# Router tables summed six pieces later, the last two weight pieces multiplied unsplit, two experts' rows fetched by one transfer, six loads moved to SyncE

## The chip, the cores and the metric

One core of a Trainium2 chip runs the kernel; the other cores are idle. The metric is device time in microseconds, the median of several executions.

## The reference, cut to what matters

Two blocks of a network for 512 tokens of width 1024, all in fp32. The first is a modulated norm, a wide projection, a retention branch and a convolution branch, and an output projection. The second is sliding-window attention beside a gated unit, cross attention to a memory of 256 rows, and a mixture of 32 experts. The change touches the second block, most of all its experts:

```python
def hierarchical_moe(h, w_router_group, w_router_expert, w1, w3, w2):
    ...
    p_group = jax.nn.softmax(xf @ w_router_group, axis=-1)      # 4 groups
    g_idx = jnp.argmax(p_group, axis=-1)
    ...
    top_logit, top_idx = lax.top_k(local, TOP_K)                # 2 of the group's 8 experts
    gate = jax.nn.softmax(top_logit, axis=-1) * g_w[:, None]
    ...
    def run_block(args):                                        # each expert on its own tokens
        xblk, e = args
        hid = jax.nn.silu(xblk @ w1[e]) * (xblk @ w3[e])
        return hid @ w2[e]
    ...
    y = jnp.zeros((T + 1, D)).at[slot_tok].add(yb * slot_w[:, None])[:T]
```

## The kernel before, in words

**Products.** An fp32 operand is cut into a high and a low part: ScalarE casts (`wh`, lines 151 and 1270), VectorE subtracts (`wl`, lines 152 and 1273), and TensorE (PE) multiplies the parts (`mm`, line 143). SyncE (SP) issues the weight loads, mostly 1 MB each, in the order of use, and issues one as soon as the buffer it goes to is free.

**Attention stage.** Around 780 to 930 us the kernel loads small tables on GpSimd's queue: a row of gains `rows` (line 823), the gate's bias `sgb` (826) and matrices `sgw` (828). GpSimd then multiplies `sgw` by a triangle in four steps (line 831). Between these it takes reciprocal roots `rs` for the norms (line 227), for which VectorE waits. Further loads on its queue are a gain row (975), `cqg` (1034), the router's weights `wr` (1102), and zeros written behind the output (1130). In this stage a scheduler of the framework places the instructions of GpSimd and the other engines.

**Experts.** From about 1050 us on each of 32 experts has three matrices of 2 MB (`w1`, `w3`, `w2`), each cut into four pieces. The list `pieces` runs w1 ×4, w3 ×2, w2 of the expert before ×2, w3 ×2, w2 ×2. One load (`piece_load`) brings two pieces into a slot of a ring of nine. The loop at line 1684 takes one piece `i` after the other; `prepare` loads and splits 5, then 4, and near the end 3 pieces ahead. One piece of each `w1` (`whole`, line 1541) is not split but multiplied in fp32 by `up_whole`. `after(i, d, f)` queues a function for the end of piece `i + d`. From here on the code's order is every compute engine's order (`manual_schedule`).

An expert has up to 64 tokens here (`CAP` per pass; overflow goes to a loop behind, which stays as it is). Tokens and gates of each expert are put into tables in DRAM by eight indirect scatters of GpSimd (`table`, line 1508, at piece 4), read back by four transfers (`table_back`, line 1513, at piece 11), and summed by six VectorE instructions (`table_sum`, lines 1518 to 1525, at piece 18) into gates `tg` and token numbers `ti`. The first four experts don't need them: their rows are picked by small matmuls. For expert 4 and later GpSimd fetches the 64 rows by one indirect transfer (`fetch`, line 1638, into one of the two buffers of `rows`, tile X4); PE turns them (`turn`, `s_turn`, line 230); ScalarE and VectorE split them (`s_parts`). `down` multiplies by `w2`; `combine` weighs the result (lines 1574 and 1575) and GpSimd adds it to the output by an indirect transfer (line 1576), each of which waits until the one before has landed.

```python
        if i == 18:
            table_sum()
...
            if c == 1 and NE <= e + 1 < 32:
                after(i, 0, lambda e=e: s_turn(e + 1))
                after(i, 1, lambda e=e: s_parts(e + 1))
            if c == 3 and NE <= e + 2 < 32:
                after(i, 0, lambda e=e: s_fetch(e + 2))
```

Of the kernel before, what the change touches and what calls it, by code (L numbers as in the profile page):

```python
# [111 lines left out]
def build(tc, I, out):  # L112
# [712 lines left out]
    sgb = ap_.tile([128, 8], F32, name="sgb")  # L825
    G.dma_start(sgb, I["sgbt"])
    sgw = ap_.tile([128, 8, 128], F32, name="sgw")
    G.dma_start(sgw, I["sgwt"])
    for j in range(4):
# [144 lines left out]
    g_out = alt("gain")  # L974
    G.dma_start(g_out, I["onorm"].to_broadcast([128, D]))
    mT = []
# [56 lines left out]
    cqg = ap_.tile([128, 256], F32, name="cqg")  # L1033
    G.dma_start(cqg, I["rows"][:, 648:].to_broadcast([128, 256]))
    oT = []
# [65 lines left out]
    wr = alt("gain", (128, KT, 40))  # L1101
    G.dma_start(wr, I["wr"])
    for k in range(KT):
# [25 lines left out]
    V.memset(zero[:64], 0.0)  # L1129
    G.dma_start(out[T:T + 64, :], zero[:64])  # L1130

# [383 lines left out]
    def table_sum():  # L1515

        t = rows[:64, 1, 512:512 + CAP]
        V.tensor_reduce(t, rows[:64, 1, :NT * CAP].rearrange("p (m v) -> p v m", m=NT), AX.X, OP.add)
        t = t.rearrange("p (e v) -> p e v", v=2)
        for l in range(2):  # L1520
            V.tensor_copy(tg[l * 64:l * 64 + 64], t[:, :, 1])
        u = rows[:64, 1, 640:672]
        V.tensor_scalar(u, t[:, :, 0], 0.0, float(1 << 20), OP.is_equal, OP.mult)
        V.scalar_tensor_tensor(u, t[:, :, 0], 1.0, u, op0=OP.subtract, op1=OP.add)
        V.tensor_copy(ti[:64], u)


# [13 lines left out]
    def whole(i):  # L1541

        n, e, c = pieces[i]
        return n == "w1" and (c == 2 or e == 0 and c == 3)

    def down(yb, hd, f, w):

        for q in range(2):
            mm(yb[q], hd[:, f], w[1][:, q, :], f == 0, False)
            mm(yb[q], hd[:, f], w[0][:, q, :], False, f == 3)  # L1550

    def add_parts(b, aS, q):
# [87 lines left out]

    def turn(x):

        b = pget("pg")
        for k in range(KT):
            transpose(b[:, k * 64:k * 64 + 64], x[:, k * 128:k * 128 + 128])
        return b.rearrange("p (k s) -> p k s", k=KT)
# [5 lines left out]
    def s_fetch(e):  # L1652
        fetch(rows[:64, e % 2], ti[:64, e:e + 1])

    def s_turn(e):
        st[e]["xb"] = turn(rows[:64, e % 2])

# [26 lines left out]
    for i, (n, e, c) in enumerate(pieces):  # L1684
# [14 lines left out]
        if i == 4:  # L1699
            rows = lp.tile([128, 2, D], F32, name="X4")  # L1700
            G.memset(rows[:64], 0.0)
            table()
        if i == 11:
            g.finish()
            table_back()
        if i == 18:
            table_sum()
        if n != "w2":
            if c == 0:
                s_[n] = pget("pa")  # L1710
            if whole(i):
                up_whole(s_[n], s_["xg"], 2 * c, raw_of[i])
            else:
                up(s_[n], s_["xg"], 2 * c, split_of.pop(i))
        else:
            if c == 0:
                s_["y"] = [pget("pg" if e == 31 else "py") for _ in range(2)]
            down(s_["y"], s_["hd"], c, split_of.pop(i))
        raw_of.pop(i)
        if c == 3:  # L1720
# [14 lines left out]
        if n == "w1" and e < 32:  # L1735
            if c == 1 and NE <= e + 1 < 32:
                after(i, 0, lambda e=e: s_turn(e + 1))
                after(i, 1, lambda e=e: s_parts(e + 1))
            if c == 3 and NE <= e + 2 < 32:
                after(i, 0, lambda e=e: s_fetch(e + 2))  # L1740
        for f in late.pop(i, ()):
# [15 lines left out]
    with tc.For_i(0, nv, 1):  # L1757
# [22 lines left out]
        fetch(rows[:64, 0], ga.ii[:, 0:1])  # L1780
        parts(turn(rows[:64, 0]), ga.xg[0])
        w1, w3, w2 = (I[n][bass.ds(ev, 1)].rearrange("o k n -> (o k) n") for n in ("w1_2", "w3_2", "w2_2"))
# [44 lines left out]
```

## Time and profile before

| | |
|---|---|
| runs | 1702.79, 1703.10, 1703.52 us, median 1703.1 |
| profiled execution | 1703.71 us, of which its span (first to last instruction) 1701.9 |
| PE busy | 1620.8 us (95%), weight loads 1265.4 beside |
| VectorE (DVE) busy | 1269.3 us (75%) |
| ScalarE (ACT) busy | 876.4 us (51%) |
| GpSimd (POOL) busy | 200.7 us (12%) |
| granted PE clock | 0.984 of full speed over the span |
| DMA | 338 MB, 202 GB/s over the span |

The busy shares are means over unlike stages, so they are read together with the page's 40 slices: there PE is at nine or more tenths almost everywhere, the DMA engines reach nine tenths from about 1200 us on, and there is one slice (the 28th, 1149 to 1191 us) in which the granted clock shows 7. Idle time in a row, "[9.89 <-DMA X<-slots]", stands before that instruction on its engine and names what ended it.

### The profile page before, as it was taken

Reading aid. Unit: us, or ns where it says so; the run is one execution under the profiler, and the core shown is the slowest. Engines: PE = TensorE matmul, PEld = TensorE weight load, DVE = VectorE, ACT = ScalarE, POOL = GpSimd, SP = SyncE. Lnnn points to the kernel's source line nnn. Section 1 sums busy time; section 2 is a strip of 40 time slices with the busy share of each in tenths; the row PEclk is TensorE's granted clock in tenths of the full one; section 3 lists DMA queues with packets and bytes.
Section 4 is the critical chain, followed back from the end, with each engine's and each line's share of the span. In section 5 each row is a group of like instructions: output and inputs, shape, how many; then the busy total and the mean of one; then the engine's idle time right before and its main releaser. Section 6 shows DMA issues by size and latency. Waiting matters only on the chain.

```text
span 1701.9 us, 20349 instructions
## 1 busy us (share of the span) xinstructions
PE 1620.8 (95%) x7587; PEld 1265.4 (74%) x7587; DVE 1269.3 (75%) x1809; ACT 876.4 (51%) x1299; POOL 200.7 (12%) x179
## 2 busy tenths in 40 slices
PE   8999999999999999999899999987999999999994
PEld 6888888888888878887787877865666666666663
DVE  5969996479994374446765554476999999998995
ACT  6533232322222334344554343356888888887884
POOL 1100100000100000004101010015112122121211
PEclk9999999999999999999999999997999999999997
DMA  9932222223222262334121331466999999999992
GB/s 342 322 104 96 97 93 99 83 91 112 79 99 89 91 230 100 118 123 142 50 75 66 112 98 50 161 228 222 381 395 403 399 394 399 389 398 394 393 368 60
DMA packets 101316, 338.02 MB, mean 199 GB/s; under 512 B 9601, under 2 KB 27329, under 8 KB 76896
## 3 DMA queue, kind: packets, MB, share of 16 engines
q1 hardware_dynamic: 90272, 308.76, 48.3%
q0 software_dynamic: 9504, 23.65, 4.9%
q10 hardware_dynamic: 1440, 4.31, 0.7%
q8 instruction: 60, 0.98, 0.2%
q14 instruction: 40, 0.33, 0.1%
HBM read 327.29 MB, written 17.11 MB: 202 GB/s over the span
## 4 chain that ended last, share of the span: by engine, by line
issue 21%; PE 17%; DMA 16%; DVE 5%; POOL 2%; ACT 2%; POOLq 0%; ACTq 0%; DVEq 0%
DMA out_dram<-xs,ti 13%; PE pmm L143 8%; PE ps L143 4%; PE ppv L143 2%; DMA out_dram<-xs,ii 2%; PE psc L143 2%; POOL rs L227 1%; PE ptr L230 1%; DMA slots<-dat,pi 0%; POOL sgw L831 0%; DMA adg<-in_w_ada_dram 0%; DVE X L755 0%; DVE xs L1180 0%; DVE wl L152 0%; DVE xs L765 0%
## 5 line engine op out<-in xcount | busy, mean ns | idle before, releaser
L151 ACT CAST wh<-raw 128x1024 fp32r<-128x1024 f32 x174 | 182.0, 1051 | 393.3 <-PE ps L143 341.6
L152 DVE TENSOR_TENSOR wl<-raw,wh 128x1024 fp32r<-128x1024 f32 x174 | 211.8, 1220 | 173.2 <-ACT wh L151 172.3
L143 PE MATMUL pmm<-wl,xr 128*128 128x512 f32 x388 | 175.6, 453 | 12.2 <-DVE wl L1273 10.3
L143 PE MATMUL pmm<-wh,X 128*128 128x512 f32 (+1 forms) x544 | 179.5, 401 | 0.3 <-DVE qn L858 0.3
L143 PE MATMUL ps<-hH,wl 128*128 128x512 f32 x448 | 176.1, 394 | 0.0
L143 PE MATMUL ps<-hL,wh 128*128 128x512 f32 x448 | 174.6, 390 | 0.0
L143 PE MATMUL ps<-hH,wh 128*128 128x512 f32 x448 | 174.5, 389 | 0.0
L491 DVE SCALAR_TENSOR_TENSOR cvo<-apad,cw,cvo 128x512 f32<-128x512 f32 x240 | 169.2, 743 | 0.9
L1273 DVE TENSOR_TENSOR wl<-X,wh 128x1024 fp32r<-128x1024 f32 x138 | 161.4, 1220 | 4.3 <-ACT wh L1270 4.0
L143 PE MATMUL pmm<-wh,xr 128*128 128x512 f32 x388 | 154.3, 398 | 0.0
L1270 ACT CAST wh<-X 128x1024 fp32r<-128x1024 f32 x138 | 138.1, 1053 | 5.6 <-DMA X<-in_w_dram 4.3
L143 PE MATMUL ps<-wl,hH 128*128 128x512 f32 x320 | 124.6, 390 | 0.0
L1273 DVE TENSOR_TENSOR wl<-raw,wh 128x1024 fp32r<-128x1024 f32 x104 | 121.6, 1220 | 3.9 <-ACT wh L1270 3.6
L143 PE MATMUL ps<-wh,hH 128*128 128x512 f32 x320 | 124.5, 390 | 0.0
L143 PE MATMUL ps<-wh,hL 128*128 128x512 f32 x320 | 124.5, 390 | 0.0
L143 PEld LDWEIGHTS pmm<-wl,xr 128*128 128x128 f32 x388 | 73.7, 190 | 61.6 <-DVE wl L1273 42.5
L143 PEld LDWEIGHTS pmm<-wh,X 128*128 128x128 f32 x544 | 102.1, 191 | 20.2 <-DVE qn L858 0.4
L143 PE MATMUL pmm<-wl,X 128*128 128x512 f32 (+1 forms) x272 | 108.4, 399 | 0.0
L1270 ACT CAST wh<-raw 128x1024 fp32r<-128x1024 f32 x104 | 104.3, 1052 | 5.2 <-DMA raw<-in_w_dram 5.0
L1576 POOL DMA_INDIRECT out_dram<-xs,ti x27 | 61.5, 2276 | 355.5 <-DVE xs L1575 355.5
L143 PEld LDWEIGHTS ps<-hH,wl 128*128 128x128 f32 x448 | 84.6, 189 | 17.5 <-issue 0.2
L143 PEld LDWEIGHTS ps<-hL,wh 128*128 128x128 f32 x448 | 84.3, 188 | 17.7 <-issue 0.2
(450 smaller groups left out, 3300.7 us busy)
## 6 DMA issues: line engine op xcount, KB each, us to landing
X<-in_w_dram SPq DMA_DIRECT2D x81, 1024.0 KB, 12.3
raw<-in_w_dram SPq DMA_DIRECT2D x63, 1024.0 KB, 11.9
raw<-in_w_in_dram SPq DMA_DIRECT2D x43, 1024.0 KB, 4.9
pre<-in_w_dram SPq DMA_DIRECT2D x42, 1024.0 KB, 11.9
adar<-in_w_ada_dram SPq DMA_DIRECT2D x16, 512.0 KB, 8.1
raw<-in_w_in_dram SPq DMA_DIRECT2D x16, 512.0 KB, 4.5
raw<-in_w_ret_out_dram SPq DMA_DIRECT2D x8, 1024.0 KB, 4.9
raw<-in_w_out_dram SPq DMA_DIRECT2D x8, 1024.0 KB, 5.0
```

The source lines that it names most:

```text
L143: PE.matmul(o, l, r, start=start, stop=stop)
L151: A.copy(hi, src)
L152: E.tensor_sub(lo, src, hi.bitcast(F32))
L227: G.tensor_tensor(o, o, mhalf[:, :w], op=OP.pow)
L230: PE.transpose(o, i, ident[:i.shape[0], :i.shape[0]])
L491: V.scalar_tensor_tensor(st["o"], ap[:, j:j + T], cw[:, k, j:j + 1], st["o"], op0=OP.mult, op1=OP.add)
L1270: A.copy(split_of[i][0], raw_of[i])
L1273: E.tensor_sub(split_of[i][1], raw_of[i], split_of[i][0].bitcast(F32))
L1576: G.indirect_dma_start(out=out, out_offset=bass.IndirectOffsetOnAxis(ap=idx[:, :1], axis=0), in_=y[:64, :], in_offset=None, bounds_check=T ...
```

## The change

1. `table_sum` runs at piece 24, not 18. A seventh instruction in it writes the token numbers of experts 1 to 31, one column to the left, into partitions 64 to 127 of `ti`.
2. With that, one indirect transfer of 128 rows brings the rows of experts `e` and `e + 1` (`e` even): one transfer every second expert in place of one each. The odd expert's rows lie in partitions 64 to 127 and are turned from there. A pair's buffer is used alternately, as an expert's was. The first one is issued at the end of piece 24. The clearing of `rows` covers 128 partitions.
3. The last two pieces of the last expert's `w2` are not split; when both are there, `down_whole` multiplies them in fp32, by output half.
4. Six loads and writes of GpSimd's queue (lines 826, 828, 972, 1034, 1102, 1130 before) go to SP's.

On DVE, in the experts' stage, before (`X_8731` is the tile `rows`, `jk` belongs to the bookkeeping of overflow, `wl` and `gain` are low parts of weights):

```order
L1273 TENSOR_TENSOR wl_8932<-X_8921,wh_8931 128x1024
L1518 TENSOR_REDUCE X_8731<-X_8731 64x64
L1521 COPY tg<-X_8731 64x32 x2
L1523 TENSOR_SCALAR X_8731<-X_8731 64x32
L1524 SCALAR_TENSOR_TENSOR X_8731<-X_8731 64x32
L1525 CAST ti<-X_8731 64x32
L1672 COPY jk<-psc 32x128
L1673 TENSOR_SCALAR jk<-jk 32x128
L1675 SCALAR_TENSOR_TENSOR jk<-jk 32x128 x6
L1273 TENSOR_TENSOR wl_8974<-pre_8963,wh_8973 128x1024
```

and with the change:

```order
L1687 COPY npre<-psc 128x33
L1688 CAST nblk<-npre 128x1
L1273 TENSOR_TENSOR wl_9013<-raw_9010,wh_9012 128x1024
L1273 TENSOR_TENSOR wl_9021<-raw_9010,wh_9020 128x1024
L1518 TENSOR_REDUCE X_8731<-X_8731 64x64
L1521 COPY tg<-X_8731 64x32 x2
L1523 TENSOR_SCALAR X_8731<-X_8731 64x32
L1524 SCALAR_TENSOR_TENSOR X_8731<-X_8731 64x32
L1525 CAST ti<-X_8731 64x32
L1526 CAST ti<-X_8731 64x31
L1273 TENSOR_TENSOR wl_9044<-raw_9041,wh_9043 128x1024
```

The overflow's bookkeeping, five weight splits and an expert's `hidden` and `combine` now stand ahead of the sum.

On POOL, in the experts' stage, before (`X_8731<-xscr` is the fetch of rows, `out_dram<-xs` the sum into the output):

```order
L1638 DMA X_8731<-xscr,ti 64x1024
L1576 DMA out_dram<-xs_9274,ii 576x1024
L1638 DMA X_8731<-xscr,ti 64x1024
L1576 DMA out_dram<-xs_9421,ii 576x1024
L1638 DMA X_8731<-xscr,ti 64x1024
```

and with the change:

```order
L1583 DMA out_dram<-xs_8982,ii 576x1024
L1645 DMA X_8731<-xscr,ti 128x1024
L1583 DMA out_dram<-xs_9128,ii 576x1024
L1583 DMA out_dram<-xs_9272,ii 576x1024
L1645 DMA X_8731<-xscr,ti 128x1024
L1583 DMA out_dram<-xs_9419,ii 576x1024
```

A fetch of 128 rows follows every second sum into the output.

On POOL, in the attention stage (a difference; `sgw` and `sgb` belong to the gated unit, `rs` are norms' roots, `gain_6769` is the gain row of the output norm):

```order
 L823 DMA rows<-in_rows_dram 128x904
-L826 DMA sgb<-in_sgbt_dram 128x8
-L828 DMA sgw<-in_sgwt_dram 128x1024
+L831 TENSOR_TENSOR sgw<-sgw,cst 128x256 x3
 L227 TENSOR_TENSOR rs_5787<-rs_5787,mhalf 128x1
 L227 TENSOR_TENSOR rs_5837<-rs_5837,mhalf 128x1
-L831 TENSOR_TENSOR sgw<-sgw,cst 128x256 x4
-L975 DMA gain_6769<-in_onorm_dram 128x1024
+L831 TENSOR_TENSOR sgw<-sgw,cst 128x256
 L227 TENSOR_TENSOR rs_5928<-rs_5928,mhalf 128x2
```

Three of the four multiplications of `sgw` now stand ahead of two roots. The loads reappear on SP between weight loads.

The diff:

```diff
@@ -823,9 +823,9 @@
     G.dma_start(rows, I["rows"].to_broadcast([128, 904]))
     qg, kg, sink, sgn = rows[:, :64], rows[:, 64:128], rows[:, 128:136], rows[:, 136:648]
     sgb = ap_.tile([128, 8], F32, name="sgb")
-    G.dma_start(sgb, I["sgbt"])
+    nc.sync.dma_start(sgb, I["sgbt"])
     sgw = ap_.tile([128, 8, 128], F32, name="sgw")
-    G.dma_start(sgw, I["sgwt"])
+    nc.sync.dma_start(sgw, I["sgwt"])
     for j in range(4):
         js = slice(2 * j, 2 * j + 2)
         G.tensor_mul(sgw[:, js], sgw[:, js], cst[:, None, C_SGU:C_SGU + 128].to_broadcast([128, 2, 128]))
@@ -972,7 +972,7 @@
         us.append(u)
     ws = block([W2[:, 1280:1792]])
     g_out = alt("gain")
-    G.dma_start(g_out, I["onorm"].to_broadcast([128, D]))
+    nc.sync.dma_start(g_out, I["onorm"].to_broadcast([128, D]))
     mT = []
     for m in range(NT):
         b = pmm()
@@ -1031,7 +1031,7 @@
     vS = ap_.tile([128, 2, D], F32, name="vS")
     nc.sync.dma_start(vS.rearrange("p a b -> p (a b)"), vscr)
     cqg = ap_.tile([128, 256], F32, name="cqg")
-    G.dma_start(cqg, I["rows"][:, 648:].to_broadcast([128, 256]))
+    nc.sync.dma_start(cqg, I["rows"][:, 648:].to_broadcast([128, 256]))
     oT = []
     for nb in range(2):
         ws = block([I["w_cq_2"][:, nb * 512:nb * 512 + 512]])
@@ -1099,7 +1099,7 @@
     V.tensor_copy(trib[:, :128], cst[:, C_TRI:C_TRI + 128])
     V.tensor_copy(trib[:, 128:], onesf)
     wr = alt("gain", (128, KT, 40))
-    G.dma_start(wr, I["wr"])
+    nc.sync.dma_start(wr, I["wr"])
     for k in range(KT):
         V.tensor_scalar(wr[:, k, :], wr[:, k, :], vcol("norm_ffn_2", k), None, OP.mult)
     iota32 = cst[:, C_E32:C_E32 + 32]
@@ -1127,7 +1127,7 @@
     g_ffn = gain(I["gffn"])
     zero = alt("xs")
     V.memset(zero[:64], 0.0)
-    G.dma_start(out[T:T + 64, :], zero[:64])
+    nc.sync.dma_start(out[T:T + 64, :], zero[:64])
 
     for m in range(NT):
         nc.sync.dma_start(slots[m].rearrange("(p s) v -> p (s v)", p=64), zero[:64, :CAP])
@@ -1523,6 +1523,7 @@
         V.tensor_scalar(u, t[:, :, 0], 0.0, float(1 << 20), OP.is_equal, OP.mult)
         V.scalar_tensor_tensor(u, t[:, :, 0], 1.0, u, op0=OP.subtract, op1=OP.add)
         V.tensor_copy(ti[:64], u)
+        V.tensor_copy(ti[64:, :31], u[:, 1:])
 
 
     def up(b, x, k0, w):
@@ -1541,13 +1542,19 @@
     def whole(i):
 
         n, e, c = pieces[i]
-        return n == "w1" and (c == 2 or e == 0 and c == 3)
+        return n == "w1" and (c == 2 or e == 0 and c == 3) or n == "w2" and e == 31 and c > 1
 
     def down(yb, hd, f, w):
 
         for q in range(2):
             mm(yb[q], hd[:, f], w[1][:, q, :], f == 0, False)
             mm(yb[q], hd[:, f], w[0][:, q, :], False, f == 3)
+
+    def down_whole(yb, hd, fs, ws):
+
+        for q in range(2):
+            for f, w in zip(fs, ws):
+                mm(yb[q], hd[:, f].bitcast(F32), w[:, q, :], False, f == 3)
 
     def add_parts(b, aS, q):
 
@@ -1638,11 +1645,11 @@
         G.indirect_dma_start(out=o, out_offset=None, in_=xscr, in_offset=bass.IndirectOffsetOnAxis(ap=ids, axis=0),
                              bounds_check=T - 1, oob_is_err=False)
 
-    def turn(x):
+    def turn(x, p):
 
         b = pget("pg")
         for k in range(KT):
-            transpose(b[:, k * 64:k * 64 + 64], x[:, k * 128:k * 128 + 128])
+            PE.transpose(b[:, k * 64:k * 64 + 64], x[p:p + 64, k * 128:k * 128 + 128], ident[p:p + 64, p:p + 64])
         return b.rearrange("p (k s) -> p k s", k=KT)
 
     def parts(b, xg):
@@ -1650,10 +1657,10 @@
         V.tensor_sub(xg[:, :, 64:], b, xg[:, :, :64].bitcast(F32))
 
     def s_fetch(e):
-        fetch(rows[:64, e % 2], ti[:64, e:e + 1])
+        fetch(rows[:, e // 2 % 2], ti[:, e:e + 1])
 
     def s_turn(e):
-        st[e]["xb"] = turn(rows[:64, e % 2])
+        st[e]["xb"] = turn(rows[:, e // 2 % 2], e % 2 * 64)
 
     def s_parts(e):
         st[e]["xg"] = xgs.next()
@@ -1698,12 +1705,12 @@
             gates()
         if i == 4:
             rows = lp.tile([128, 2, D], F32, name="X4")
-            G.memset(rows[:64], 0.0)
+            G.memset(rows, 0.0)
             table()
         if i == 11:
             g.finish()
             table_back()
-        if i == 18:
+        if i == 24:
             table_sum()
         if n != "w2":
             if c == 0:
@@ -1715,8 +1722,12 @@
         else:
             if c == 0:
                 s_["y"] = [pget("pg" if e == 31 else "py") for _ in range(2)]
-            down(s_["y"], s_["hd"], c, split_of.pop(i))
-        raw_of.pop(i)
+            if not whole(i):
+                down(s_["y"], s_["hd"], c, split_of.pop(i))
+            elif c == 3:
+                down_whole(s_["y"], s_["hd"], (2, 3), (raw_of[i - 1], raw_of[i]))
+        if not (n == "w2" and e == 31 and c == 2):
+            raw_of.pop(i)
         if c == 3:
             if n == "w1":
                 after(i, 1, lambda e=e: s_copy1(e))
@@ -1736,8 +1747,8 @@
             if c == 1 and NE <= e + 1 < 32:
                 after(i, 0, lambda e=e: s_turn(e + 1))
                 after(i, 1, lambda e=e: s_parts(e + 1))
-            if c == 3 and NE <= e + 2 < 32:
-                after(i, 0, lambda e=e: s_fetch(e + 2))
+            if c == 3 and e % 2 == 0 and NE <= e + 2 < 32:
+                after(i, 1 if e == 2 else 0, lambda e=e: s_fetch(e + 2))
         for f in late.pop(i, ()):
             f()
     p8.close()
@@ -1778,7 +1789,7 @@
         ga.start()
         ga.finish()
         fetch(rows[:64, 0], ga.ii[:, 0:1])
-        parts(turn(rows[:64, 0]), ga.xg[0])
+        parts(turn(rows[:, 0], 0), ga.xg[0])
         w1, w3, w2 = (I[n][bass.ds(ev, 1)].rearrange("o k n -> (o k) n") for n in ("w1_2", "w3_2", "w2_2"))
         aS = lp.tile([128, 2, 512], F32, name="gain0")
         b = pget("ph")
```

## Rows read from the trace of the kernel before

**Rows 1.** Busy time by stretch: us, each engine's busy time, granted clock, DMA share, GB/s.

```profile
1162.00:1170.00 8.00, 7.45 (x35) 5.00 (x33) 2.83 (x3) 2.38 (x4) 6.22 (x4) 1.00 1.01 419
1170.00:1182.00 12.00, 2.68 (x6) 1.66 (x6) 6.24 (x19) 1.87 (x4) 1.57 (x3) 0.62 0.20 60
1182.00:1206.00 24.00, 21.99 (x95) 17.31 (x96) 22.36 (x24) 20.46 (x26) 7.54 (x4) 0.84 0.86 313
1206.00:1640.00 434.00, 420.22 (x1888) 285.17 (x1887) 408.47 (x421) 362.96 (x473) 84.40 (x52) 1.00 1.02 395
```

**Rows 2.** Timeline of DVE: start us, busy us, line, operation, [idle before <-what ended it].

```profile
1159.08 5.75 DVE L1273 TENSOR_TENSOR wl<-X,wh 128x1024 fp32r<-128x1024 f32 x5
1174.72 0.58 DVE L1518 TENSOR_REDUCE X<-X 64x64 f32<-64x256 f32 x1 [9.89 <-DMA X<-slots]
...
1176.23 0.27 DVE L1672 COPY jk<-psc 32x128 f32<-32x128 f32 x1
...
1185.43 6.90 DVE L1273 TENSOR_TENSOR wl<-raw,wh 128x1024 fp32r<-128x1024 f32 x6
```

**Rows 3.** Timeline of SP's queue: two loads that follow each other.

```profile
1164.86 0.33 SPq L1260 DMA_DIRECT2D X<-in_w_dram  x1
1179.84 0.33 SPq L1264 DMA_DIRECT2D pre<-in_w_dram  x1
```

**Rows 4.** Timeline of POOL: two of the table's eight scatters.

```profile
1147.34 3.22 POOL L1508 DMA_INDIRECT slots<-dat,pi  x1 [7.11 <-DVE dat L1505]
...
1157.81 7.88 POOL L1508 DMA_INDIRECT slots<-dat,pi  x1 [0.30 <-issue]
```

**Rows 5.** Timeline of POOL: a sum into the output and the fetch behind it.

```profile
1216.21 2.28 POOL L1576 DMA_INDIRECT out_dram<-xs,ii  x1 [12.68 <-DVE xs L1575]
1218.80 0.98 POOL L1638 DMA_INDIRECT X<-xscr,ti  x1 [0.30 <-PE pmm L143]
```

**Rows 6.** Timeline of DVE in the same stretch.

```profile
1215.97 2.36 DVE L1273 TENSOR_TENSOR wl<-raw,wh 128x1024 fp32r<-128x1024 f32 x2
1218.36 0.69 DVE L1650 TENSOR_TENSOR xr<-psc,xr 128x512 fp32r<-128x512 f32 x1
```

**Rows 7.** All 28 fetches of line 1638, from issue to landing.

```profile
DMA to landing us min/median/max: 5.7/8.3/9.3
```

**Rows 8.** Timeline of PE: the turning of the rows fetched in rows 5.

```profile
1229.84 0.71 PE L230 MATMUL psc<-ident,X 64*128 64x64 f32 x8
```

**Rows 9.** DMA issues on the page: a weight load's KB and median us to landing.

```profile
raw<-in_w_dram SPq DMA_DIRECT2D x63, 1024.0 KB, 11.9
```

**Rows 10.** Timeline of DVE at the end.

```profile
1678.27 1.22 DVE L1273 TENSOR_TENSOR gain<-pre,xs 128x1024 fp32r<-128x1024 f32 x1
1679.52 1.54 DVE L1575 SCALAR_TENSOR_TENSOR xs<-ptr,tg,xs 64x512 f32<-64x512 f32 x2
...
1683.86 1.54 DVE L1575 SCALAR_TENSOR_TENSOR xr<-psc,tg,xr 64x512 f32<-64x512 f32 x2 [1.54 <-ACT xr L1574]
```

**Rows 11.** Timeline of POOL at the end: experts 30 and 31.

```profile
1681.34 2.26 POOL L1576 DMA_INDIRECT out_dram<-xs,ti  x1 [15.06 <-DVE xs L1575]
1686.65 1.41 POOL L1576 DMA_INDIRECT out_dram<-xr,ti  x1 [3.04 <-DMA out_dram<-xs,ti]
```

**Rows 12.** Timeline of PE: an unsplit piece of expert 31, and a split one.

```profile
1661.29 1.88 PE L143 MATMUL pmm<-raw,xr 128*128 128x512 f32 x4
...
1679.54 0.50 PE L143 MATMUL psc<-gain,hd 128*128 128x512 f32 x1
```

**Rows 13.** Timeline of POOL in the attention stage.

```profile
792.28 1.99 POOL L227 TENSOR_TENSOR rs<-rs,mhalf 128x1 f32<-128x1 f32 x2 [4.68 <-DVE rs L225]
794.25 5.48 POOL L831 TENSOR_TENSOR sgw<-sgw,cst 128x256 f32<-128x256 f32 x4
```

**Rows 14.** Timeline of DVE in the attention stage.

```profile
801.03 0.29 DVE L858 TENSOR_TENSOR kn<-psc,rs 128x128 f32<-128x128 f32 x1 [1.98 <-POOL rs L227]
```

**Rows 15.** Timeline of SP in the attention stage: three loads from here to 840 us.

```profile
788.56 51.89 SPq L167 DMA_DIRECT2D raw<-in_w_in_dram  x3
```

## The prediction

> **What bounds the kernel now.** I read the busy time by stretch first, since a mean over the whole span hides which engine sets which stage. From 1206 to 1640 us [rows 1] PE is busy 420.2 of 434.0 us and DVE 408.5, and the DMA engines are full (share 1.02, 395 GB/s): three resources near their limit, so work taken from one of them alone is worth little there. The stretch 1170 to 1182 is different: PE 2.7 of 12 us, DVE 6.2, DMA share 0.20, granted clock 0.62. Nothing is full, so something waits. DVE's timeline says for what [rows 2]: five splits end at 1159.08 + 5.75 = 1164.83, and the table's sum starts at 1174.72, after 9.89 us of idle that the read-back of the slots ended. DVE runs in program order, so everything behind the sum stood still: no split weights for PE, no buffer free, and SP issued no load from 1164.86 to 1179.84 [rows 3]. [...] This is a wait for data on the engine that feeds all the others, so its length goes into the end time one for one.
>
> Why was the read-back late? On POOL [rows 4] one of the eight scatters took 7.88 us, from 1157.81 to 1165.69. It ended 0.86 us after DVE's splits had ended. Much the same is seen in small later on: a sum into the output took 2.28 us, from 1216.21 to 1218.49, and the fetch behind it 0.98 [rows 5]; the longer one lies over two splits, which end at 1218.33, and the short one starts beside an operation whose first input is PSUM [rows 6]. So POOL's indirect transfers seem to be held while DVE subtracts from SBUF to SBUF.
>
> **The later sum.** The work that now stands ahead of it is what ran from 1176.23 to the second of the six splits that start at 1185.43 [rows 2]: 1185.43 + 2 × 6.90 / 6 − 1176.23 = 11.5 us. DVE had that work to do anyhow; it moves up into the idle time. It starts at 1164.83 in place of 1176.23, and DVE comes to the sum at 1164.83 + 11.5 = 1176.3. The slots were there at 1174.72, 1.6 us earlier. If they still are, the whole 9.9 us go: **−9.9**. The seventh instruction costs what the six cost each, (1176.23 − 1174.72) / 6: **+0.25**.
>
> Are there transfers to keep up? Over the stretches with the hole the DMA engines had 12 × 0.80 + 24 × 0.14 = 13.0 us of idle time [rows 1], more than the 9.9. Since the buffers come free as DVE and PE move up, the loads move up with them.
>
> But the slots' time is not given. In the stall POOL worked without DVE beside it: a scatter and four reads of the slots. Now DVE's splits and the overflow's instructions run there. Lower bound of what that costs: nothing, ready at 1174.72, no wait. Upper bound: three of POOL's remaining steps held by as much as the sum into the output was against the fetch [rows 5], 3 × (2.28 − 0.98) = 3.9, thus 1178.6; and the last read-back behind one 1 MB load on engines that are now full, 1.05 MB / 395 GB/s = 2.65 [rows 1, 9], thus 1181.3, a wait of 5.0. I take the three held steps without the load, since the held steps have a row close by in kind and time and the queueing has none: 1178.6 − 1176.3 = **+2.3**.
>
> [...]
>
> **The pair of rows.** Per two experts one fetch goes (28 become 14, 0.98 us of POOL each [rows 5], an engine at 84.4 of 434 us [rows 1]: nothing). The bytes are the same. The one question is whether a transfer of 128 rows lands in time for the first of the two experts. A single fetch lands after 8.3 us in the median, 9.3 at most [rows 7]; that issued at 1218.80 is used by PE at 1229.84 [rows 5, 8], 11.04 us later. Lower bound for the pair: 256 KB more at 395 GB/s, 8.3 + 0.7 = 9.0, in time. Upper bound: everything but the issue doubles, 0.98 + 2 × 7.3 = 15.6, late by 4.6. Between them, a 1024 KB load lands in 11.9 [rows 9], so on a line from 256 KB and 8.3 the 512 KB stand at 9.5, or 10.5 from the largest single one: inside 11.04. The pair fetch is issued at the same place in the loop as its first expert's was, its odd expert gets an expert's time more, and the buffer it goes to was last turned two experts earlier. I take **0**. The first pair, issued at piece 24, has nine pieces to its use at piece 33; at 434 us per 27 experts of 12 pieces [rows 1] that is 12 us, and DVE is some pieces ahead of PE besides. The clearing of twice the partitions comes ahead of a stretch in which POOL waited 7.11 us for DVE [rows 4]: 0.
>
> **The tail.** DVE does not split the last two pieces. Before, it did one split (1678.27) ahead of expert 30's weighing (1679.52), so that comes 1679.52 − 1678.27 = 1.25 earlier [rows 10]; POOL's sum of expert 30 starts 1.25 earlier, and expert 31's, which waits for its landing (3.04 of idle [rows 11]), too: 1685.4. That holds if expert 31's own values are there. PE takes the two pieces whole, by 1.88 each [rows 12], from 1679.54 on: 1683.3. The second half's two operations follow (1683.86 + 1.54 ends DVE's two halves before [rows 10], after a later PE), so 1685.1 at most, before 1685.4. **−1.25**; between 0, if PE's limb is later by more than I see, and −1.5.
>
> **Six transfers to SP.** On POOL each issue took about half a microsecond, on an engine that is idle 88% of the time. In the attention stage SP issues three loads between 788.56 and 840 [rows 15], so two small ones between them find SP free, and the same holds of the other four, whose consumers come later. What moves is the scheduler's order: three of the four `sgw` steps (5.48 / 4 = 1.37 each) now stand ahead of a pair of roots [rows 13]. POOL sat idle for 4.68 us there, which covers the 4.1, if `sgw` has landed when it is idle; if it comes 3 us later, the roots are late by as much. On the other side, an issue ahead of a root for which DVE waited 1.98 [rows 14] is gone: −0.6. I take **0**, within −0.6 to +3.
>
> **Sum.** On the profiled execution: 1703.7 − 9.9 + 0.25 + 2.3 − 1.25 + 0 + 0 = 1695.1. That execution is 0.6 above the median of the runs, 1703.1, so the forecast is **1694.5**. Without the returned wait it would be 1692.2, with all of the upper bound 1697.2.
>
> **Rivals.** About 0.2%, 3.4 us, is what a measurement of this kernel can tell from no change; faster means below 1699.7, slower above 1706.5.
>
> *The wait comes back at the new place.* POOL is held in all its steps as in the 7.88 us of rows 4, not as in rows 5: with one such hold (7.88 − 0.98 = 6.9) the slots come at 1181.6 and DVE waits 5.3, with a load in front 8.0: 1697.5 to 1700.2. For it: the one long scatter. Against it: between the splits ahead of the new place there are operations that read PSUM or a single input, and there POOL came through [rows 5, 6]. 0.13, of which 0.10 still is faster.
>
> *The pair lands late* (the slower side). Point from which it decides: PE has 434.0 − 420.2 = 13.8 us of idle in some 27 experts, 1.0 a pair, to absorb [rows 1]; beyond that each pair's lateness is lost, 14 times. With a gain of 8.6 the kernel is even at 8.6 / 14 + 1.0 = 1.6 us late, a landing of 12.7. A landing of 13.5, midway in the bounds' upper part, is late by 2.5: 1.5 × 14 = 21, thus 1715. For it: every second expert's DVE and PE would stand. Against it: the 1024 KB that land in 11.9 [rows 9]. 0.06, half of it slower (0.04), the rest spread.
>
> *The attention stage loses.* `sgw` on SP's queue lands late and the roots wait the full 3 us: 1697.5, still faster. 0.06.
>
> *The stall's removal does not reach the end*: the transfers of the last stage set the end, and only the tail's 1.25 is left, 1701.9. Against it: the 13.0 us of free DMA time. 0.05, the same. Or the slots are ready early and nothing waits: 1692.2, part of the forecast.
>
> **The numbers.** The forecast (the wait at the new place between 0 and 5) 0.70; the rivals 0.13, 0.06, 0.06, 0.05. The range takes in the forecast with its bounds (1692.2 − 0.6 − 0.25 on the low side, 1691.3, to 1697.2), the loss in the attention stage, and of the returned wait all up to 1699: 1691.0 to 1699.0. Faster 0.70 + 0.10 + 0.06 + 0.01 = 0.87; same 0.03 + 0.01 + 0.05 = 0.09; slower 0.04.
>
> **What would show it.** Right: the idle ahead of the table's sum is under 5 us, SP's gap of 15 us is gone, the DMA share of 1170 to 1182 is above 0.7, and PE's clock stays at its upper level. The turn of an even expert follows PE's other work without a wait for the fetch, whose landing is 9 to 11 us. At the end DVE goes from expert 30's weighing to expert 31's with no split between, and the two sums into the output follow as before, 1.25 us sooner against the stage. Wrong: idle of 5 us or more ahead of the sum with the slots as releaser; PE waiting for the fetch in every second expert; or the hole closed, and the same time found again as waits for loads behind 1500 us, which would say that the transfers had set the end all along.

## The result, and the profile after

The changed kernel takes 1680.3 us (four executions, 1679.9 to 1681.5) against 1703.3, a ratio of 0.986 with a 95% interval of 0.9846 to 0.9874: 23 us less. The forecast was 1694.5, which is 8.6 us less than before. Its sign was right, its size was not. On a second chip the changed kernel took 1684.1 us and the kernel before 1703.5, so each run below is compared by its ratio to the kernel before, run beside it on the same chip.

The two profiled executions have spans of 1701.9 and 1679.7, 22.2 us apart. To see where, I take one instruction that stands once in each expert, the product of its hidden values on DVE, for experts 0, 2, 21 and 31. In the kernel before (timeline of DVE):

```profile
1152.74 0.42 DVE L1562 TENSOR_TENSOR hs<-hs,ppv 128x256 f32<-128x256 f32 x1 [0.28 <-ACT hs L1561]
...
1196.65 0.42 DVE L1562 TENSOR_TENSOR hs<-hs,ppv 128x256 f32<-128x256 f32 x1 [0.37 <-ACT hs L1561]
...
1505.64 0.42 DVE L1562 TENSOR_TENSOR hs<-hs,ppv 128x256 f32<-128x256 f32 x1
...
1675.29 0.42 DVE L1562 TENSOR_TENSOR hs<-hs,ppv 128x256 f32<-128x256 f32 x1
```

and in the changed kernel:

```profile
1151.12 0.42 DVE L1569 TENSOR_TENSOR hs<-hs,ppv 128x256 f32<-128x256 f32 x1 [0.28 <-ACT hs L1568]
...
1186.84 0.42 DVE L1569 TENSOR_TENSOR hs<-hs,ppv 128x256 f32<-128x256 f32 x1 [0.32 <-ACT hs L1568]
...
1495.78 0.41 DVE L1569 TENSOR_TENSOR hs<-hs,ppv 128x256 f32<-128x256 f32 x1
...
1656.70 0.42 DVE L1569 TENSOR_TENSOR hs<-hs,ppv 128x256 f32<-128x256 f32 x1
```

The lead grows from 1.6 to 9.8 us between experts 0 and 2 (the hole), stays there until expert 21, and grows to 18.6 by expert 31. What is left of the 22.2 lies behind that: 1.8 up to the last output transfer and 1.8 after it. So the hole gave 8.2, nearly what was forecast (7.4), and the largest other part, 8.7, came from a stage of which the forecast expected nothing. The 1.6 us ahead of expert 0 can't be counted on: in the second profile of the changed kernel (below) expert 0 comes 2.2 us later than in the kernel before.

The stretches that answer to [rows 1], in the changed kernel:

```profile
1162.00:1170.00 8.00, 7.34 (x34) 4.93 (x32) 7.06 (x16) 3.80 (x7) 5.75 (x5) 1.00 0.97 358
1170.00:1182.00 12.00, 7.35 (x31) 5.36 (x32) 9.92 (x17) 8.68 (x10) 5.61 (x5) 0.96 0.82 287
1182.00:1206.00 24.00, 24.00 (x112) 17.39 (x110) 22.28 (x24) 18.17 (x26) 2.35 (x1) 0.95 0.92 357
1206.00:1640.00 434.00, 426.90 (x1919) 290.46 (x1919) 415.02 (x428) 370.05 (x482) 75.38 (x40) 1.00 1.01 403
```

The DMA share in the hole rose from 0.20 to 0.82 and PE's granted clock was 0.96 there, where it was 0.62 before, as the prediction said. The last row is the surprise: 403 GB/s where [rows 1] has 395. The same stretch of the kernel before, cut in two at 1500 us, shows what the row of 434 us hid:

```profile
1206.00:1500.00 294.00, 289.16 (x1303) 196.78 (x1301) 280.90 (x291) 249.91 (x327) 58.45 (x36) 1.00 1.02 397
1500.00:1640.00 140.00, 131.06 (x586) 88.39 (x586) 127.57 (x132) 113.06 (x147) 25.95 (x16) 1.00 1.02 390
```

PE idles 4.8 of 294 us in the first part and 8.9 of 140 in the second. Experts 22 to 29 took 16.6 to 18.0 us there and 16.26 each in the changed kernel. The reason stands in the page's DMA issues of the changed kernel, to be read against [rows 7, 9]:

```profile
raw<-in_w_dram SPq DMA_DIRECT2D x63, 1024.0 KB, 8.7
...
X<-xscr,ti POOLq DMA_INDIRECT x14, 9.3
```

A weight load lands after 8.7 us in the median, not 11.9. How this runs through the stage is told by the loads to `raw` in two stretches. The kernel before, 1206 to 1300 us and 1500 to 1640:

```profile
DMA to landing us min/median/max: 7.1/8.6/9.2
```

```profile
DMA to landing us min/median/max: 18.8/20.2/22.2
```

and the changed kernel:

```profile
DMA to landing us min/median/max: 6.9/7.7/8.3
```

```profile
DMA to landing us min/median/max: 8.9/9.3/9.5
```

In the kernel before the loads fell behind by some 0.6 us per expert (20.2 − 8.6 = 11.6 us over some 19 experts). That their lead was used up about expert 21, behind which the periods grow from 16.26 to 16.6 us and more, is a reading.

The hole itself, on DVE (answers to [rows 2]) and POOL ([rows 4]) of the changed kernel:

```profile
1172.47 2.36 DVE L1273 TENSOR_TENSOR wl<-raw,wh 128x1024 fp32r<-128x1024 f32 x2
1176.67 0.59 DVE L1518 TENSOR_REDUCE X<-X 64x64 f32<-64x256 f32 x1 [1.84 <-DMA X<-slots]
```

```profile
1155.33 8.87 POOL L1508 DMA_INDIRECT slots<-dat,pi  x1 [0.30 <-issue]
1164.50 1.08 POOL L1508 DMA_INDIRECT slots<-dat,pi  x1 [0.30 <-issue]
1165.89 1.77 POOL L1508 DMA_INDIRECT slots<-dat,pi  x1 [0.30 <-issue]
```

The idle ahead of the sum is 1.84 us (2.3 forecast) in place of 9.89. The one long scatter is that of [rows 4] at the same place, beside the same splits, 8.87 us in place of 7.88; the two behind it took 1.08 and 1.77 us, where both took 0.97. GpSimd's last two reads of the slots, before and then changed:

```profile
1172.02 1.03 POOL L1513 DMA_DIRECT2D X<-slots  x2 [1.11 <-DMA slots<-dat,pi]
```

```profile
1171.52 1.03 POOL L1513 DMA_DIRECT2D X<-slots  x2 [1.08 <-DMA slots<-dat,pi]
```

Measured from expert 0's product, GpSimd issued them 1.1 us later than before. The sum started 4.1 us behind them, where it was 1.7 before, so another 2.4 us went into the landing. The DMA engines were 0.82 busy then and not 0.20; that the loads are what delayed it is a reading.

### The profile page after: what moved, and what is told of

Its sections match the earlier page's. It is cut to its first block, busy times and chain, and to the rows that moved or that the text cites. A ratio compares the mean times of both kernels' runs of the same rounds, so it can differ in the third digit from the quotient of the medians.

```text
span 1679.7 us, 20298 instructions
## 1 busy us (share of the span) xinstructions
PE 1619.1 (96%) x7587; PEld 1261.8 (75%) x7587; DVE 1265.9 (75%) x1808; ACT 873.9 (52%) x1297; POOL 186.2 (11%) x159
## 5 line engine op out<-in xcount | busy, mean ns | idle before, releaser
L143 PEld LDWEIGHTS pmm<-wh,X 128*128 128x128 f32 x544 | 101.0, 189 | 20.2 <-DVE qn L858 0.4
L143 PEld LDWEIGHTS ps<-hH,wh 128*128 128x128 f32 x448 | 84.1, 188 | 17.5
```

The source lines that it names most:

```text
L143: PE.matmul(o, l, r, start=start, stop=stop)
```

## The experiments

**The four parts alone.** Each is put into the kernel before.

```diff
-        if i == 18:
+        if i == 24:
             table_sum()
```

(and the first single fetch one piece later)

> Before with the later sum alone (and the first single fetch one piece later, since it needs the sum). The changed kernel gained 8.2 us at the hole and 8.8 us more in experts 22 to 29, where the kernel before had periods of 16.6 to 18.0 us in place of 16.26. Theory A (the pair fetch gives the late gain): only the hole closes, 1703 - 8 = 1695, and experts 22 to 29 still run at about 17.3 us. Theory B (the hole's removal gives it: the loads that were not issued in the hole are missing later): 1703 - 8 - 9 = 1686, with 16.26 us per expert up to the end.

Measured: 0.9940 (0.9927 to 0.9954), 10 us. In the trace, which is of the slowest of the six executions, the lead grows by 7.3 us in the hole and by nothing after; experts 21 to 30 take 155.1 us, as in the kernel before. Theory A.

The pair alone: the second cast of `ti`, `fetch` of 128 rows, `turn` from the half, every second expert.

> Before with the pair fetch alone; the sum stays at piece 18 with its seventh instruction. Theory A: the hole stays (9 to 10 us of idle on DVE) and the late stage runs at 16.26 us per expert, 1703 - 9 = 1694. Theory B: nothing but the seventh instruction, 1703, and experts 22 to 29 as slow as before. The prediction's slower rival (the pair lands late): 1715 or more, with PE waiting for the fetch in every second expert.

Measured: 0.9949 (0.9936 to 0.9961). The hole is there, and experts 21 to 30 take 146.4 us: 8.7 less. Theory A again, and the slower rival is out: the 14 fetches land after 9.3 us in the median in the changed kernel, against the 9.5 worked out.

The six transfers alone, `G.dma_start` to `nc.sync.dma_start`:

> Before with the six transfers on SP alone. The trace of the changed kernel is 4.0 us ahead after the attention stage, 0.6 of it from the start of the program and 2.9 from two stretches in which PE did not fall to its lower clock, and loses 2.4 of it again ahead of the experts, also by the clock. Theory C (the gain is real work saved on GpSimd's path to VectorE): 1.5 to 4 us faster, 1699 to 1701.5. Theory D (only the clock's falls came elsewhere, no steady gain): within 1 us of 1703, with falls at other places.

Measured: 0.998 (0.9969 to 0.9991), 3.4 us. The busy time by stretch in the attention stage, before and then with the transfers on SP:

```profile
800.00:830.00 30.00, 23.36 (x134) 19.72 (x132) 17.34 (x46) 11.43 (x35) 6.80 (x8) 0.94 0.11 37
830.00:870.00 40.00, 39.06 (x213) 32.41 (x212) 28.75 (x58) 24.01 (x57) 5.65 (x3) 0.96 0.25 80
```

```profile
800.00:830.00 30.00, 26.45 (x168) 22.53 (x167) 18.59 (x49) 13.57 (x40) 5.86 (x6) 1.00 0.06 24
830.00:870.00 40.00, 39.07 (x217) 32.19 (x216) 27.67 (x56) 23.69 (x57) 5.65 (x3) 1.00 0.24 80
```

and DVE's wait that answers to [rows 14]:

```profile
799.85 0.29 DVE L858 TENSOR_TENSOR kn<-psc,rs 128x128 f32<-128x128 f32 x1 [0.82 <-POOL rs L227]
```

1.2 us come from the wait for POOL (0.82 in place of 1.98), and 0.5 from a shorter end of the program (last section). In this profile some 3 us more come from PE, whose granted clock is 1.00 in both stretches. It falls in them in the profiles of the kernel before (0.94 and 0.96; it shows 0.50 from 811.2 to 814.2 us and from 845.4 to 848.4), of the sum alone and of the pair alone (0.89 and 1.00 each) and of the tail alone (1.00 and 0.96; next). But that isn't shown to be the transfers' doing: of the sixteen profiles with the six transfers on SP, ten have such a fall. The second profile of the changed kernel is one of them:

```profile
800.00:830.00 30.00, 25.58 (x152) 22.01 (x151) 17.95 (x47) 11.82 (x35) 6.57 (x8) 0.94 0.17 64
830.00:870.00 40.00, 38.56 (x200) 32.09 (x200) 29.39 (x57) 22.34 (x52) 5.65 (x3) 0.92 0.24 79
```

So theory C is shown as to the wait. The clock's part comes and goes from one execution to the next, as in theory D, and what of the 3.4 us (1.5 to 5.3) is beyond 1.7 stays open.

The last two pieces unsplit alone:

> Before with the last two pieces unsplit alone. The prediction's step: the sum of expert 30 starts 1.25 us earlier and all behind it, 1702. In the changed kernel the last output transfer started 1.8 us earlier against the last expert's hidden values, since expert 30's output transfer took 1.42 us in place of 2.26 with no split beside it: 1701.3. If the end behind the last output transfer is shorter for the same reason (13.5 in place of 15.25 us in the trace of the changed kernel), 1699.5.

Measured: 0.9995 (0.9986 to 1.0003). The trace shows the 1.8 us between the last hidden values and the last output transfer (9.54 in place of 11.36), but that run lost 0.8 in the starved stage ahead of it. The gain is within what can be told here. Together the four make 0.9940 − 0.0051 − 0.0020 − 0.0005 = 0.9864, where 0.986 was measured: within the intervals the parts add up.

**What is dear in the single fetches?** All of these start from the changed kernel; experts 21 to 30 take 146.3 us in it.

One fetch of 64 rows per expert again:

> The changed kernel with one fetch of 64 rows per expert again, all else as changed. If the pair fetch alone gives the late gain: 1680 + 8 to 9 = 1689, landing of the weight loads growing from 8 to 20 us as in the kernel before, and experts 22 to 29 at about 17.3 us. If the gain needs the open queue after the closed hole: 1680 to 1682.

As before, but an odd expert's rows go to the upper partitions:

```diff
-        fetch(rows[:, e // 2 % 2], ti[:, e:e + 1])
+        p = e % 2 * 64
+        fetch(rows[p:p + 64, e // 2 % 2], ti[:64, e:e + 1])
```

> The changed kernel with one fetch of 64 rows per expert, but an odd expert's rows go to partitions 64 to 127. Theory P (a transfer to the lower 64 partitions loads the 16 DMA engines unevenly, and the weight loads wait for the busiest): upper and lower half take turns, the mean is even, and the time is the changed kernel's, 1680, with loads landing in 8 us all along. Theory N (each indirect transfer has a price of its own, so 28 cost more than 14): as with single fetches to one half, 1689, and loads landing later and later.

The pair by two transfers, `for p in (0, 64)`, at the pair's place:

> The changed kernel with the pair fetched by two transfers of 64 rows, one behind the other at the pair's place, one for each half of the partitions. Theory P: 1680, as one transfer. Theory N: 28 transfers again, 1689.

Thirteen small transfers more, for odd experts:

```diff
+            if c == 3 and e % 2 == 1 and NE < e + 1 < 32:
+                after(i, 0, lambda e=e: fetch(rows[:2, (e + 1) // 2 % 2], ti[:2, e + 1:e + 2]))
```

> The changed kernel with 13 more indirect fetches of two rows each (8 KB), one for each second expert, which bring rows that are there already. With 64-row fetches to either half, and with two back to back, the weight loads fell behind; with one of 128 rows they don't. Theory N1 (the price is one per transfer, whatever its rows): 27 transfers again, loads landing in up to 20 us, experts 22 to 29 at 17 us or more, 1688 and more. Theory N2 (the price goes by rows or shape: a transfer of 64 rows moves its bytes less well than one of 128): two rows cost next to nothing, 1680.

128 half rows per expert (index 2·token + half, the view of `xscr` with rows of 512):

> The changed kernel with one fetch per expert again, but of 128 half rows (2 KB each, upper and lower half of the partitions) in place of 64 rows; PE turns them by four transposes of 128x128. 28 transfers, the same bytes, the shape of the pair. Theory S (a transfer of 128 positions is spread over the DMA engines better than one of 64): loads landing in 8 to 9 us all along, 16.26 us per expert, 1683 where the changed kernel is at 1682. Theory F (each transfer that moves real data has a price, whatever its shape): loads landing in 20 us from expert 20 on, 1690 or more.

128 positions per expert, of which the other half has indices out of bounds, alternating (`V.memset(u2[:, 1 - h::2], float(1 << 20))`):

> The changed kernel with one fetch per expert of 128 positions of 4 KB rows; for an even expert the upper 64 positions, for an odd one the lower 64 have an index out of bounds and are dropped. 28 transfers. Theory S: as the changed kernel, 1683. Theory F: 1690 or more.

and always the upper one out of bounds:

> As the run with alternating halves, but the rows of every expert lie in the lower 64 positions and the upper 64 are always dropped. Theory S1 (the position in the transfer picks the DMA engine, so the lower half always loads the same ones): the loads fall behind, 1690 or more, though alternating halves don't. Theory S2 (a transfer of 128 positions is dealt out well whichever are dropped): 1683. Theory F: 1690 or more in both.

| fetches | ratio (95%) | experts 21 to 30, us |
|---|---|---|
| 14 of 128 rows (changed kernel, second chip) | 0.9878 (0.9862 to 0.9893) | 146.4 |
| 28 of 64 | 0.9935 (0.9912 to 0.9958) | 155.8 |
| 28 of 64, odd to upper partitions | 0.9940 (0.9918 to 0.9963) | 155.0 |
| 28 of 64, two at a time | 0.9928 (0.9904 to 0.9952) | 156.3 |
| 14 of 128 and 13 of 2 | 0.9878 (0.9861 to 0.9894) | 146.4 |
| 28 of 128 half rows | 0.9883 (0.9868 to 0.9898) | 146.3 |
| 28 of 128 positions, halves alternate | 0.9895 (0.9875 to 0.9914) | 146.3 |
| 28 of 128 positions, always the lower | 0.9913 (0.9896 to 0.9929) | 150.2 |

The changed kernel was run again for this, with the expectation:

> The changed kernel again, on the chip of these runs: ratio 0.986 as before, 1680 where the kernel before is at 1703.

The loads' medians, halves alternating first, then always the lower:

```profile
raw<-in_w_dram SPq DMA_DIRECT2D x63, 1024.0 KB, 8.2
```

```profile
raw<-in_w_dram SPq DMA_DIRECT2D x63, 1024.0 KB, 11.6
```

The number of transfers isn't the price (28 can be free), nor the partitions written (row 3). At the same bytes, count and length it is the position of the rows within the transfer: always in the first 64 starves the loads, taking turns doesn't. The intervals of these two ratios overlap; it is the loads' landing and the nine experts of the traces, one profile each, that tell them apart. In a transfer of 128 the position and the partition written are one; only row 3 parts them. An expert fills only about the first half of its 64 positions (the packet records from 1206 to 1500 us hold 58 of 4 KB per expert, fetch and sum together), so what the pair does is to put every second expert's rows elsewhere in a transfer. That some DMA engines get more than others is the reading that fits, and the traces agree with it: they hold 16 steps in which each load's landing is counted, and the page counts 16 DMA engines. For loads issued from 1500 to 1640 us (those whose steps the trace can assign), median us from the issue, and how many of the 16 steps came later than 10 us:

| | eighth step | last step | steps later than 10 us, mean |
|---|---|---|---|
| kernel before (50 loads) | 7.9 | 20.5 | 7.5 |
| changed kernel (21) | 7.1 | 9.0 | 0.0 |
| halves alternate (28) | 7.1 | 9.1 | 0.0 |
| always the lower (25) | 6.5 | 19.4 | 4.0 |

About half of each starved load, or more, lands as early as ever, and the late steps hold up the whole. That a step is one engine's share is inferred, as the records don't name the engine. In the runs with dropped positions taking turns evens the load (last step 9.1 against 19.4 us); with always the lower half 4.0 of the 16 steps are late, and in the kernel before, with 64 positions, 7.5. Equal shares of neighbouring positions would come near both: by an estimate from the 58 / 2 = 29 rows of an expert they fill 29 / 8 = 3.6 of sixteen shares of 128 positions and 29 / 4 = 7.3 of sixteen of 64; no run was made to test that.

**The other indirect transfer.** From the kernel with 28 fetches of 64, the sum into the output as 128 half rows:

> The changed kernel with one fetch of 64 rows per expert (which starved the last stage: loads landing in 20 us, 0.9935 of the kernel before), and the sum into the output, from expert 4 on, as 128 half rows in place of 64 rows, for the same bytes. Theory S1 (rows in the first 64 positions always load the same DMA engines, whichever transfer it is): with the output spread the loads keep up, landing in 8 to 10 us, 16.26 us per expert to the end, 0.988 of the kernel before. If only the fetch has that property: starved as before, 0.993.

Measured: 0.9923 (0.9898 to 0.9948); from 1500 us on the loads land after 19.5 us in the median. Not relieved. But from expert 6 on each took 16.5 us here instead of 16.26, and the sum landed after 9.8 us instead of 8.5, so the sum's smaller rows have a price of their own. It neither shows nor excludes the same effect for the sum.

**Faster versions.** The sum three pieces later, and one piece later:

> The changed kernel with the sum at piece 27 and the first pair fetch three pieces later too. In the changed kernel DVE still waits 1.84 us ahead of the sum; three more splits (3.4 us) ahead of it cover this: 1.8 us faster, 1678.5, if the first pair's rows still land before PE turns them (in the changed kernel the fetch is issued at 1178.7 and PE turns at 1188.2). If they don't, PE stands for a few us once and the time is the same or up to 2 us longer.

> The changed kernel with the sum and the first pair fetch one piece later. With the sum three pieces later the wait was gone but the first pair landed 4.9 us late. One split (1.15 us) ahead of the sum fits into the 1.84 us wait and doesn't move the sum, so the fetch is where it was: 1.1 us faster than the changed kernel, if the slots are as late as there.

Three pieces: 0.9885 (0.9861 to 0.9908). No wait ahead of the sum, but the first pair comes late, the mechanism of the prediction's slower rival, once. PE's timeline there:

```profile
1191.00 1.08 PE L1652 MATMUL psc<-ident,X 64*128 64x64 f32 x8 [4.88 <-DMA X<-xscr,ti]
```

One piece: 0.9857 (0.9840 to 0.9873), beside 0.9878 (0.9862 to 0.9893) for the changed kernel, so the intervals overlap; in the traces the hole costs 1.5 and 2.0 us less than in the two traces of the changed kernel. More unsplit pieces, `e % 4 == 0` in place of `e == 0` in `whole`:

> The changed kernel with a second unsplit piece of w1 for every fourth expert: DVE and ScalarE have one split less there, PE 0.94 us more. Probe of the room that the DMA engines have left now. If DVE sets the 16.26 us per expert and the loads have room: up to 1.1 us less for each of seven experts, 1673. If PE sets it as much as DVE: 1680 or up to 5 us longer. If the DMA engines are at their limit at 403 GB/s: no gain, and loads landing later and later again.

0.9842 (0.9826 to 0.9857). Each fourth expert takes 15.54 in place of 16.26, and loads land in 12 us at the end in place of 9. So the splits on DVE and ScalarE set the period there, not PE, and the growing landing, at 408 GB/s, is read as little room left in the DMA engines. Both:

> The changed kernel with the sum one piece later and a second unsplit piece of w1 for every fourth expert, the two that were faster by themselves (0.9857 and 0.9842 of the kernel before, the changed kernel beside them 0.9878): 0.982 to 0.984, 1674 where the kernel before is at 1703.

0.9837 (0.9824 to 0.9851), 1675.7 us: faster than the kernel before. Of the changed kernel's two measurements its interval lies below the second (0.9862 to 0.9893) and overlaps the first. With every second expert and half rows in the sum:

> The version with the sum one piece later, now with a second unsplit piece of w1 for every second expert in place of every fourth (0.73 us less for each), and with the output's sums as half rows as well as the pair fetch. By theory S1 the DMA engines have more room, the loads land in under 10 us, and seven more experts gain 0.7 us: 0.980 to 0.982 of the kernel before, 1670. If the DMA engines have no more room: loads landing in 15 to 20 us near the end and no gain on 0.9837.

0.9834 (0.9813 to 0.9855), no more than that. The sums land after 9.8 us there, after 8.3 in the version before; that they take what the unsplit pieces gain is a reading.

## Why the prediction was right and wrong

In the two profiles the changed kernel gained 1.6 us ahead of expert 0, 8.2 in the hole, 8.7 in the last stage, 1.8 in the tail and 1.8 behind it; the forecast had 0, 7.4, 0, 1.25 and 0.

**The later sum** was right in that the wait could be filled, and near in size: 8.2 us in the trace of the changed kernel and 7.3 in that of the part alone, against 9.9 − 0.25 − 2.3 = 7.4. The wait that came back was 1.84, but not for the reason forecast. I took 3.9 us for three held steps of GpSimd and left out the 2.65 for a read-back behind a load; measured were 1.1 for GpSimd's steps and 2.4 for the landing. That the term came out near is luck. The first rival, one more long hold at the new place, did not come: the long scatter (8.87) is the old one.

**The pair of rows** is the step that failed. "The bytes are the same. The one question is whether a transfer of 128 rows lands in time": it landed as worked out (9.3 against 9.5), and I took 0, where it gave 8.7 us in the last stage. The bytes are the same, but not where they stand in the transfer, and that decided whether the weight loads kept up. Behind it lies the reading of [rows 1]: I took 1206 to 1640 as one stretch, saw three full resources and shared PE's 13.8 us of idle out evenly as slack. It was 4.8 in two thirds and 8.9 in the last third. The rival that the transfers of the last stage set the end had the right bound but asked only whether it would take the hole's gain away. It doesn't, as the sum alone shows: the loads move up with the rest, and experts 21 to 30 take 155.1 us with it as without it.

**Six transfers to SP**: taken as 0 within −0.6 to +3, measured −3.4. The wait for the roots lost 1.2, not 0.6, and 0.5 came at the end of the program, which was not in the sum. The rest isn't placed: the clock's falls, which were not in the sum either, differ from one execution to the next (0.94 and 0.92 in the second profile of the changed kernel from 800 to 870 us, 1.00 in the first).

**The tail**: −1.25 taken, −1.8 in the trace up to the last output transfer. The mis-sized term is expert 30's sum. It starts 1.1 us earlier against the last hidden values, and with no split beside it its instruction took 1.42 in place of 2.26 us. This answers to [rows 10, 11], the last line from DVE:

```profile
1661.61 1.42 POOL L1583 DMA_INDIRECT out_dram<-xs,ti  x1 [13.94 <-DVE xs L1582]
1666.23 1.42 POOL L1583 DMA_INDIRECT out_dram<-xr,ti  x1 [3.20 <-DVEq L1768]
```

```profile
1665.20 0.75 DVE L1582 SCALAR_TENSOR_TENSOR xr<-psc,tg,xr 64x512 f32<-64x512 f32 x1 [0.96 <-ACTq L1768]
```

So the forecast's condition failed as well: expert 31's own values, done at 1665.95, and not the landing of expert 30's sum are now what the last sum waits for.

**What was not in the sum**: the 1.8 us after the last output transfer, in the next section.

## What to carry to other kernels

Cut a long steady stretch in two or three before reading its busy shares, and look at how the loads' landing time runs through it: here its median had grown from 8.4 us (loads issued from 1206 to 1250) to 13.9 (1400 to 1450) before PE's idle time rose from 4.8 of 294 us to 8.9 of 140. Where indirect transfers run beside a saturated load stream, ask which positions of the transfer are filled, not only how many bytes it moves (8.2 and 11.6 us to a load's landing here, at the same bytes). And when work is moved ahead of a wait, add up what the data behind it can still bear: three pieces removed the wait and made PE idle 4.88 us for the first fetch, one piece took 1.5 and 2.0 us off the hole in the traces.

## What was not expected of the hardware

At the end of the program, when its last transfer has landed, GpSimd drains its queue, which took 7.34 to 8.97 us in four kernels, longer the more transfers it had issued (89 to 109). Instructions of the program's last lines, by count, min/median/max ns; the kernel before:

```profile
L1823 POOLq DRAIN  x3: 46/109/8968, 1692.1 to 1701.7; - x3
```

six plain transfers less (the kernel before with these on SP):

```profile
L1823 POOLq DRAIN  x3: 46/103/8478, 1687.0 to 1696.0; - x3
```

fourteen indirect ones less (the pair alone):

```profile
L1824 POOLq DRAIN  x3: 46/109/7825, 1681.6 to 1690.0; - x3
```

both, the changed kernel:

```profile
L1834 POOLq DRAIN  x3: 46/103/7335, 1671.5 to 1679.4; - x3
```

The longest of the three is the one that counts. That is 0.49 / 6 and 1.14 / 14, 0.08 us for each, and 1.63 for all twenty: most of the 1.8 us behind the last output transfer. GpSimd issued 109, 103, 95 and 89 transfers in these four, so the drain was 0.08 us for every one of them. The thirteen small ones brought 1.06 back (8.40). The count alone doesn't tell it all: with the sums as half rows 103 transfers drained in 4.64, where 103 took 8.48 above, and why is open.

The other is the position effect: with the bytes, the count and the length of the transfers held, where their rows stand in them moved the loads' median landing from 8.2 to 11.6 us and a stretch of nine experts by 4 us. Why 64 positions starve the stage more (9 us) than 128 with the upper half dropped is open as well.
